# A decoder trunk on one core: the products' moving operands stored as two runs, even columns and odd columns, and read in turn

## The chip, the cores and the metric

The kernel runs on one core of one Trainium2 chip. The metric is the device time of one execution in microseconds (us); less is better. The kernel before takes 568.06 us (median of 3 runs, 568.05 to 568.49).

## What is computed

Two transformer layers on 256 rows of 1024 features. Layer 0 has full causal attention with 16 heads (with one block of 256 keys the block selection selects nothing beyond the own block), layer 1 has 16 query heads on 4 shared key/value heads, a window of 128 and a learned sink. Each layer ends with a gated feed-forward part with a causal convolution of width 3.

```python
for l in range(DEPTH):                       # DEPTH = 2
    h = rmsnorm(x, attn_norm[l])
    ...                                      # q, k, v = h @ w...; rotary; attention -> o
    x = x + o @ w_o
    x = x + conv_ffn(rmsnorm(x, ffn_norm[l]), w_up[l], conv_w[l], conv_b[l], w_down[l])
return rmsnorm(x, final_norm)

def conv_ffn(h, w_up, conv_w, conv_b, w_down):
    u = h @ w_up                             # 1024 -> 2 x 2816
    up = jnp.pad(u, ((0, 0), (CONV_W - 1, 0), (0, 0)))
    u = conv_b + sum(conv_w[j] * up[:, j:j + S_] for j in range(CONV_W))
    gate, val = jnp.split(u, 2, axis=-1)
    return (jax.nn.silu(gate) * val) @ w_down
```

All data are float32, and so is the output.

## The kernel before, in words

**Products in three parts.** Every projection is made from operands split in two: `hi` is the value rounded to the type fp32r, `lo` what is left. A product of x and w is three matmuls that add up in one PSUM bank: x_hi w_hi, x_hi w_lo, x_lo w_hi. Each matmul has a stationary operand of 128x128, which TensorE loads before it, and a moving operand that it reads column by column.

**Weights.** The host packs all weights into 90 units of 128x2048 (`pack`, L1041), in the order of use. A unit is fetched by one DMA on SP (`fetch`, L151), rounded to `wh` by ScalarE (`hi_part`, L156-157), and its rest `wl` taken by VectorE (`lo_part`, L159-160), each in two or four pieces. `prepare` (L166) spreads these pieces over the planned time; `used(i)` (L188) starts unit i+4, and a unit's last step starts the fetch of unit i+3. Weight and activation tiles that TensorE reads come from `spaced` (L79), which begins each 4 elements into its tile.

**Who moves and who is stationary.** In four kinds of product the weights move and activations are stationary: `proj` (L310-323; q, k, v of layer 0 and k/v of layer 1 with 512 columns, the q groups of layer 1 with 256), `v_first` (L733-740, the first block), `Down.mm` (L521-539; attention output and feed-forward down, 512 columns), and `Down.end` (L579-597; the very last unit, in pieces of 256 columns). In the feed-forward up product (`mm` inside `ffn`, L614-630) it is the other way round: a 128x128 piece of `w_up` is stationary and the activations of all 256 rows, features on the partitions, move (256 columns). These activations are `hT` for the first `n_raw` = 4 units and `hS` for the rest.

**Where the moving activations come from.** After a block of the residual stream is final, `feats` (L260-288) transposes it with TensorE into PSUM, ScalarE copies it with the norm's gain into `y` (L276), and VectorE makes `hi` and `lo` from it (L279, L280). For the feed-forward part `feats` is called with `keep=y`; the rows' scale (`rb`) isn't known yet, so units 0 to 3 work with unscaled activations (`hT`) and scale the result, while `scale_x` (L632-643) multiplies `y` by `rb` on VectorE and splits it again into `hS`. Without `keep`, the result is a stationary operand for `proj`.

**Order.** The program's order is written by hand with a planned clock: `tick(ns)` (L116) adds the planned time of the products just issued, counted as columns / 2.4 ns each, and runs the ScalarE and VectorE steps that have come due; `chain` (L124) enqueues such steps, and `require` (L136) forces them before their result is used. In the attention parts the projections of later head groups and of the attention output are fed in as filler between the scores.

Of the kernel before, what the change touches and what calls it, by code (L numbers as in the profile page):

```python
# [60 lines left out]
def trunk(ctx: ExitStack, tc, x, xw, pos, cpk, fin, sinks, w, out):  # L61
# [37 lines left out]

    def half(n):  # L100
        return slice(n * 512, (n + 1) * 512)

# [155 lines left out]
    def feats(b, n, sets, key, keep=None):  # L260

        ts = [bank("t"), bank("t")]
        for j in range(4):
            nc.tensor.transpose(ts[j // 2][:, (j % 2) * P:(j % 2 + 1) * P],
                                xr[b][:, (4 * n + j) * P:(4 * n + j + 1) * P], ident)
        tick(450)

        def steps(hT, g, y, m):
            c = slice(2 * m, 2 * m + 2)
            hi, lo = (part[:, c, blk(b)] for part in hT[n])  # L270
            y_ = y[:, c]

            def gain():
                for j in range(2):
                    col = g + 4 * n + 2 * m + j
                    nc.scalar.activation(y_[:, j], ts[m][:, j * P:(j + 1) * P], AF.Copy, scale=cp[:, col:col + 1])  # L276

            def parts():
                nc.vector.tensor_copy(hi, y_)  # L279
                nc.vector.tensor_tensor(out=lo, in0=y_, in1=f(hi), op=ALU.subtract)  # L280

            return gain, parts

        for k, (hT, g) in enumerate(sets):
            y = mid().rearrange("p (j t) -> p j t", j=4) if keep is None else keep[n][:, :, blk(b)]
            for m in range(2):
                gain, parts = steps(hT, g, y, m)
                chain(key, (200.0 + 1000.0 * k + 500.0 * m, gain), (500.0, parts))
# [21 lines left out]
    def proj(o, hT, b, wv, units=()):  # L310

        n = o.shape[-1]
        for c in range(KC):
            require("x", b, c // 4)
            xh, xl = hx(hT, c)
            wh, wl = wv(c)
            nc.tensor.matmul(o, xh[:, blk(b)], wh, start=(c == 0), stop=False)  # L317
            nc.tensor.matmul(o, xh[:, blk(b)], wl, start=False, stop=False)  # L318
            nc.tensor.matmul(o, xl[:, blk(b)], wh, start=False, stop=(c == KC - 1))  # L319
            tick(3 * n / 2.4)  # L320
            if units and (c + 1) * len(units) % KC == 0:
                used(units[(c + 1) * len(units) // KC - 1])
            yield 3 * n / 2.4
# [190 lines left out]
    class Down:  # L514
# [6 lines left out]
        def mm(self, i, k, b, cols):  # L521
            if self.acc is None:
                self.acc = [[bank("acc") for _ in range(2)] for _ in range(NB)]
            need(self.u + i)
            self.wait(i)
            hi, lo = wq[self.u + i]
            ph, pl = self.parts[2 * i + k]
            first = i == 0 and k == 0
            end = k == 1 and (i == self.n_u - 1 or i == self.n_u - 2 and self.short and (b, cols[0][0]) == (1, 1))
            for n, c in cols:  # L530
                o = self.acc[b][n][:, c]
                s_ = slice(k * D + n * 512 + c.start, k * D + n * 512 + c.stop)
                nc.tensor.matmul(o, ph[:, blk(b)], hi[:, s_], start=first, stop=False)  # L533
                nc.tensor.matmul(o, ph[:, blk(b)], lo[:, s_], start=False, stop=False)  # L534
            for n, c in cols:
                o = self.acc[b][n][:, c]
                s_ = slice(k * D + n * 512 + c.start, k * D + n * 512 + c.stop)
                nc.tensor.matmul(o, pl[:, blk(b)], hi[:, s_], start=False, stop=end)  # L538
            tick(len(cols) * 3 * (c.stop - c.start) / 2.4)

        def units(self, lo, hi):
            for i in range(lo, hi):
                for k in range(2):
                    for b in range(NB):
                        self.mm(i, k, b, [(n, slice(0, 512)) for n in range(2)])
                        yield 6 * 512 / 2.4
                used(self.u + i)

        def finish(self, i0, after, tail=None, by_half=False):

            last = self.n_u - 1

            def unit(i, b, n):
                for k in range(2):
                    self.mm(i, k, b, [(n, slice(0, 512))])

            if by_half:
                for n in range(2):
                    for b in range(NB):
                        for i in range(i0, self.n_u):  # L560
                            unit(i, b, n)
                        self.add(b, n, after)
            for b in () if by_half else range(NB):
                for n in range(2):
                    for i in range(i0, last):
                        unit(i, b, n)
                    if b and n and tail is not None:
                        self.end(b, n, tail)
                    elif b:
                        unit(last, b, n)  # L570
                        self.add(b, n, after)
                if b == 0:
                    for n in range(2):
                        unit(last, b, n)
                        self.add(b, n, after)
            for i in range(i0, self.n_u):
                used(self.u + i)

        def end(self, b, n, tail):  # L579

            i = self.n_u - 1
            require("x", b, n)
            x_ = xr[b][:, half(n)]
            nc.vector.tensor_tensor(out=x_, in0=self.acc[b][n], in1=x_, op=ALU.add)
            need(self.u + i)
            self.wait(i)
            wh, wl = wq[self.u + i]
            for m in range(2):
                o = bank("u")[:, :S]
                for k in range(2):  # L590
                    ph, pl = (t[:, blk(b)] for t in self.parts[2 * i + k])
                    c = slice(k * D + n * 512 + m * S, k * D + n * 512 + (m + 1) * S)
                    nc.tensor.matmul(o, ph, wh[:, c], start=(k == 0), stop=False)
                    nc.tensor.matmul(o, ph, wl[:, c], start=False, stop=False)
                    nc.tensor.matmul(o, pl, wh[:, c], start=False, stop=(k == 1))
                tick(640)
                tail(m, o)

# [9 lines left out]
    def ffn(layer, u_up, u_dn, hT, y, rb, after, tail=None):  # L608
# [5 lines left out]
        def mm(i, up, cs_):  # L614
            need(u_up + i)
            hi, lo = wq[u_up + i]
            for j in range(2):
                o = up[j]
                for c in cs_:
                    if i < n_raw:  # L620
                        for b in range(NB):
                            require("x", b, c // 4)
                    else:
                        require("y", c // 2)
                    s_ = slice((2 * c + j) * P, (2 * c + j + 1) * P)
                    xh, xl = hx(hT if i < n_raw else hS, c)
                    nc.tensor.matmul(o, hi[:, s_], xh, start=(c == 0), stop=False)  # L627
                    nc.tensor.matmul(o, hi[:, s_], xl, start=False, stop=False)  # L628
                    nc.tensor.matmul(o, lo[:, s_], xh, start=False, stop=(c == KC - 1))  # L629
                    tick(3 * 256 / 2.4)  # L630

        def scale_x(m):  # L632
# [4 lines left out]
            def times():  # L637
                for b in range(NB):
                    require("rb", b)
                nc.vector.tensor_tensor(out=y_, in0=y_, in1=rb.unsqueeze(1).to_broadcast([P, 2, S]), op=ALU.mult)  # L640

            chain(("y", m), (2000.0 + 1000.0 * m, times), (700.0, lambda: nc.scalar.activation(hi, y_, AF.Copy)),
                  (600.0, lambda: nc.vector.tensor_tensor(out=lo, in0=y_, in1=f(hi), op=ALU.subtract)))
# [89 lines left out]
    def v_first(c):  # L733
# [2 lines left out]
        wh, wl = (t[:, s_] for t in wq[c // 4])  # L736
        for k, (a, m) in enumerate(((xh, wh), (xl, wh), (xh, wl))):
            for b in range(NB):
                nc.tensor.matmul(v_acc[b], a[:, blk(b)], m, start=(c == 0 and k == 0), stop=(c == KC - 1 and k == 2))  # L739
        tick(1280)  # L740

    def v_out(b, n, o):
# [298 lines left out]
def pack(inp):  # L1041
# [3 lines left out]
    def k_major(m):  # L1045
        return m.reshape(m.shape[0] // P, P, m.shape[1])

    units = []
    m = k_major(inp["w_qkv_a"][0])
    q, k, v = (m[:, :, i * D:(i + 1) * D] for i in range(3))  # L1050
    qk = [np.concatenate([q[:, :, g * 256:(g + 1) * 256], k[:, :, g * 256:(g + 1) * 256]], axis=2) for g in range(4)]
    blocks = [v[:, :, :512], qk[0], qk[1], qk[2], v[:, :, 512:], qk[3]]

    def halves(blk):
        for a in range(2):
# [2 lines left out]
    def rows2(mat):  # L1058
        mm = k_major(mat)
        for i in range(mm.shape[0] // 2):  # L1060
            units.append(mm[2 * i:2 * i + 2].transpose(1, 0, 2).reshape(P, UNIT))

    def up(mat):
        mm = k_major(mat).reshape(KC, P, 2, NF, P)
# [5 lines left out]
    rows2(inp["w_o_a"][0])  # L1070
    up(inp["w_up"][0])
    rows2(inp["w_down"][0])
    halves(k_major(inp["w_kv_b"]))

    order = [(2 * (j // 4) + e) * 4 + j % 4 for j in range(NH // 2) for e in range(2)]
    m = k_major(inp["w_q_b"][0].reshape(D, NH, HD)[:, order].reshape(D, D))
    for g in range(4):
        units.append(m[:, :, g * 256:(g + 1) * 256].transpose(1, 0, 2).reshape(P, UNIT))
    rows2(inp["w_o_b"][0].reshape(NH, HD, D)[order].reshape(D, D))
    up(inp["w_up"][1])  # L1080
    rows2(inp["w_down"][1])
# [41 lines left out]
```

## Time and profile before

| what | value |
|---|---|
| device time, median of 3 | 568.06 us |
| profiled execution: span from first to last instruction | 565.9 us |
| around that span, to the median | 2.2 us |
| TensorE matmul busy | 558.0 us, 3858 matmuls |
| VectorE busy | 427.7 us |
| ScalarE busy | 379.6 us |
| GpSimd busy | 101.6 us |
| mean granted TensorE clock | 0.996 |
| weight fetches | 90 of 1024 KB, 4.8 us from issue to landing |

How to read it: matmuls are pipelined, so the time of one row (for example 275 ns) is longer than the distance between the starts of two of them (about 113 ns in the same place). What a stream of products costs is read from the starts, and this distance is called the pitch below. The profile's rows give a shape as partitions x elements and the number of times after an x; a row of waits names who waited, for whom, and how long in all.

### The profile page before, as it was taken

What the parts mean: (1) busy time and instruction counts of PE and PEld (TensorE: products, weight loads), DVE (VectorE), ACT (ScalarE), POOL (GpSimd) and SP (SyncE); (2) the same over time, 40 slices, a digit from 0 to 9 for tenths busy, and PEclk for the clock granted to TensorE, in tenths of its full rate; (3) what the DMA queues carried; (4) which work ended last, traced back from release to release, by engine and by line L of the source; (5) the groups of instructions that cost most, each with busy time, mean ns of one, the idle gap of its engine ahead of it and who ended that gap; (6) DMA issues with size and microseconds to landing.
All of it is one profiled execution on the core that took longest, in us unless ns stands there. A gap on an engine that the chain in (4) does not pass through costs nothing.

```text
span 565.9 us, 10192 instructions
## 1 busy us (share of the span) xinstructions
PE 558.0 (99%) x3858; PEld 504.4 (89%) x3858; DVE 427.7 (76%) x928; ACT 379.6 (67%) x768; POOL 101.6 (18%) x124
## 2 busy tenths in 40 slices
PE   9999999999999999999999999999999999999995
PEld 7888888899999999988888988889999999988884
DVE  6798678589798888755369988788888888873414
ACT  6988777578577776743449798877657777664213
POOL 7321001012323222100001000002332333110003
PEclk9999999999999999999999999999999999999998
DMA  8974344442566566555542724142465555765201
GB/s 328 371 281 155 145 149 150 149 149 76 197 215 204 213 215 224 207 199 189 216 156 85 289 76 150 74 150 76 149 250 197 206 203 204 254 215 213 85 0 74
DMA packets 15311, 100.99 MB, mean 178 GB/s; under 512 B 1952, under 2 KB 2080, under 8 KB 3744
## 3 DMA queue, kind: packets, MB, share of 16 engines
q1 hardware_dynamic: 14976, 100.09, 49.4%
q8 instruction: 30, 0.49, 0.3%
q10 hardware_dynamic: 288, 0.26, 0.1%
q14 instruction: 17, 0.14, 0.1%
HBM read 99.30 MB, written 1.05 MB: 177 GB/s over the span
## 4 chain that ended last, share of the span: by engine, by line
PE 93%; ACT 3%; DVE 3%; issue 1%; POOL 0%; DVEq 0%; POOLq 0%; ACTq 0%
PE acc L533 9%; PE acc L534 9%; PE acc L538 9%; PE u L628 6%; PE u L627 6%; PE u L629 6%; PE t L628 6%; PE t L629 6%; PE t L627 6%; PE acc L317 4%; PE acc L319 4%; PE acc L318 4%; PE acc L739 2%; PE acc L627 2%; PE acc L628 2%; PE acc L629 2%
## 5 line engine op out<-in xcount | busy, mean ns | idle before, releaser
L160 DVE TENSOR_TENSOR wl<-wr,wh 128x1024 fp32r<-128x1024 f32 (+1 forms) x208 | 222.2, 1086 | 65.9 <-ACT wh L157 65.4
L157 ACT ACTIVATE wh<-wr 128x1024 fp32r<-128x1024 f32 (+1 forms) x208 | 189.8, 946 | 69.7 <-PE acc L538 55.5
L671 POOL TENSOR_TENSOR m<-m,m 128x256 f32<-128x256 f32 x44 | 64.7, 1470 | 176.3 <-DVE m L666 129.0
L533 PE MATMUL acc<-wh,q 128*128 128x512 f32 x238 | 94.5, 397 | 0.2 <-ACT q L492 0.2
L534 PE MATMUL acc<-wl,q 128*128 128x512 f32 x238 | 92.9, 391 | 0.0
L627 PE MATMUL u<-q,wh 128*128 128x256 f32 x320 | 88.4, 277 | 0.0
L628 PE MATMUL u<-q,wh 128*128 128x256 f32 x320 | 88.2, 276 | 0.0
L629 PE MATMUL u<-q,wl 128*128 128x256 f32 x320 | 88.0, 275 | 0.0
L629 PE MATMUL t<-q,wl 128*128 128x256 f32 x288 | 79.2, 275 | 0.0
L627 PE MATMUL t<-q,wh 128*128 128x256 f32 x288 | 79.2, 275 | 0.0
L628 PE MATMUL t<-q,wh 128*128 128x256 f32 x288 | 79.2, 275 | 0.0
L538 PE MATMUL acc<-wh,q 128*128 128x512 f32 x238 | 77.1, 389 | 0.0
L628 PEld LDWEIGHTS u<-q,wh 128*128 128x128 f32 x320 | 60.1, 188 | 0.0
L629 PEld LDWEIGHTS u<-q,wl 128*128 128x128 f32 x320 | 60.1, 188 | 0.0
L627 PEld LDWEIGHTS u<-q,wh 128*128 128x128 f32 x320 | 59.9, 188 | 0.0
L317 PE MATMUL acc<-wh,q 128*128 128x512 f32 (+1 forms) x160 | 57.1, 357 | 0.0
L319 PE MATMUL acc<-wh,q 128*128 128x512 f32 (+1 forms) x160 | 55.4, 346 | 0.0
L318 PE MATMUL acc<-wl,q 128*128 128x512 f32 (+1 forms) x160 | 55.2, 345 | 0.0
L627 PEld LDWEIGHTS t<-q,wh 128*128 128x128 f32 x288 | 54.1, 188 | 0.0
L628 PEld LDWEIGHTS t<-q,wh 128*128 128x128 f32 x288 | 54.1, 188 | 0.0
L629 PEld LDWEIGHTS t<-q,wl 128*128 128x128 f32 x288 | 54.1, 188 | 0.0
L533 PEld LDWEIGHTS acc<-wh,q 128*128 128x128 f32 x238 | 44.7, 188 | 9.7 <-ACT q L492 0.7
(167 smaller groups left out, 991.3 us busy)
## 6 DMA issues: line engine op xcount, KB each, us to landing
wr<-in_w SPq DMA_DIRECT2D x90, 1024.0 KB, 4.8
first<-in_xw SPq DMA_DIRECT2D x5, 384.0 KB, 5.6
xr<-in_x SPq DMA_DIRECT2D x2, 512.0 KB, 8.2
first<-in_xw SPq DMA_DIRECT2D x1, 768.0 KB, 7.0
fin_t<-in_fin SPq DMA_DIRECT2D x1, 512.0 KB, 6.0
out<-ot SPq DMA_DIRECT2D x1, 512.0 KB, 2.6
first<-in_xw SPq DMA_DIRECT2D x1, 388.0 KB, 3.5
out<-m ACTq DMA_DIRECT2D x1, 256.0 KB, 2.1
```

What stands on the lines that cost most here:

```text
L157: nc.scalar.activation(wq[i][0][:, c], raws[i][:, c], AF.Copy)
L160: nc.vector.tensor_tensor(out=wq[i][1][:, c], in0=raws[i][:, c], in1=f(wq[i][0][:, c]), op=ALU.subtract)
L317: nc.tensor.matmul(o, xh[:, blk(b)], wh, start=(c == 0), stop=False)
L318: nc.tensor.matmul(o, xh[:, blk(b)], wl, start=False, stop=False)
L319: nc.tensor.matmul(o, xl[:, blk(b)], wh, start=False, stop=(c == KC - 1))
L533: nc.tensor.matmul(o, ph[:, blk(b)], hi[:, s_], start=first, stop=False)
L534: nc.tensor.matmul(o, ph[:, blk(b)], lo[:, s_], start=False, stop=False)
L538: nc.tensor.matmul(o, pl[:, blk(b)], hi[:, s_], start=False, stop=end)
L627: nc.tensor.matmul(o, hi[:, s_], xh, start=(c == 0), stop=False)
L628: nc.tensor.matmul(o, hi[:, s_], xl, start=False, stop=False)
L629: nc.tensor.matmul(o, lo[:, s_], xh, start=False, stop=(c == KC - 1))
L671: nc.gpsimd.tensor_tensor(out=h, in0=gs, in1=t[1], op=ALU.mult)
```

## The change

The moving operands of all projections get another order in memory: of n columns that one product reads, the n/2 even ones lie first, then the n/2 odd ones. The product's access pattern then takes one element of the first run, one of the second, and so on, so that the columns come in their old order and land in PSUM where they did. The number, sizes and order of all instructions stay.

```diff
+    def turns(t, n=None, at=0):
+        t = t.rearrange("p (a i) -> p i a", a=2)
+        return t if n is None else t[:, at // 2:(at + n) // 2]
+    def pairs(o):
+        return o.rearrange("p (i a) -> p i a", a=2)
+    def turned(t, b):
+        return t.rearrange("p c (a b i) -> p c a b i", a=2, b=NB)[:, :, :, b]
...
-            hi, lo = (part[:, c, blk(b)] for part in hT[n])
+            hi, lo = (part[:, c, blk(b)] if keep is None else turned(part[:, c], b) for part in hT[n])
...
-                    nc.scalar.activation(y_[:, j], ts[m][:, j * P:(j + 1) * P], AF.Copy, scale=cp[:, col:col + 1])
+                    t = ts[m][:, j * P:(j + 1) * P]
+                    nc.scalar.activation(y_[:, j], t if keep is None else t.rearrange("p (i a) -> p a i", a=2), AF.Copy,
+                                         scale=cp[:, col:col + 1])
...
+        o = pairs(o)
...
-            wh, wl = wv(c)
+            wh, wl = (turns(t) for t in wv(c))
...
+            for o, s_ in part:
+                nc.tensor.matmul(o, ph[:, blk(b)], turns(hi[:, s_]), start=first, stop=False)
+                nc.tensor.matmul(o, ph[:, blk(b)], turns(lo[:, s_]), start=False, stop=False)
+            for o, s_ in part:
+                nc.tensor.matmul(o, pl[:, blk(b)], turns(hi[:, s_]), start=False, stop=end)
...
-                    xh, xl = hx(hT if i < n_raw else hS, c)
+                    xh, xl = (turns(t) for t in hx(hT if i < n_raw else hS, c))
...
-                nc.vector.tensor_tensor(out=y_, in0=y_, in1=rb.unsqueeze(1).to_broadcast([P, 2, S]), op=ALU.mult)
+                r = rb.rearrange("p (i a) -> p a i", a=2).unsqueeze(1).to_broadcast([P, 2, 2, P])
+                ya = y_.rearrange("p c (a i) -> p c a i", a=2)
+                nc.vector.tensor_tensor(out=ya, in0=ya, in1=r, op=ALU.mult)
...
-                nc.tensor.matmul(v_acc[b], a[:, blk(b)], m, start=(c == 0 and k == 0), stop=(c == KC - 1 and k == 2))
+                nc.tensor.matmul(pairs(v_acc[b]), a[:, blk(b)], turns(m), start=(c == 0 and k == 0), stop=(c == KC - 1 and k == 2))
```

`Down.end` reads pieces of 256 columns out of a 512-column block in the same way. The host puts the weights in the new order: `pack` gets a function `turns(m, n=512)` that is applied to the q, k, v, k/v and output and down weights (to the q groups of layer 1 with n = 256); the up weights are stationary and stay as they are. The feed-forward activations get the order on the chip: with `keep`, the ScalarE copy out of the transposes (L276) reads every other column from PSUM and writes runs of 64; `scale_x` reads `rb` at every other column. Transposes, scores, the attention's products with v, and their operands are not touched.

More of the change, by code (lines that the diff above doesn't have):

```diff
@@ L284, in feats @@
         for k, (hT, g) in enumerate(sets):
-            y = mid().rearrange("p (j t) -> p j t", j=4) if keep is None else keep[n][:, :, blk(b)]
+            y = mid().rearrange("p (j t) -> p j t", j=4) if keep is None else turned(keep[n], b)
             for m in range(2):
@@ L528, in mm @@
             first = i == 0 and k == 0
[L529 to L539, printed above, removed]
+            end = k == 1 and (i == self.n_u - 1 or i == self.n_u - 2 and self.short and (b, cols[0]) == (1, 1))
+            part = [(pairs(self.acc[b][n]), slice(k * D + n * 512, k * D + (n + 1) * 512)) for n in cols]
+            for o, s_ in part:
[3 more added lines that the diff above has]
+                nc.tensor.matmul(o, pl[:, blk(b)], turns(hi[:, s_]), start=False, stop=end)
+            tick(len(cols) * 3 * 512 / 2.4)
         def units(self, lo, hi):
@@ L544, in units @@
                     for b in range(NB):
-                        self.mm(i, k, b, [(n, slice(0, 512)) for n in range(2)])
+                        self.mm(i, k, b, range(2))
                         yield 6 * 512 / 2.4
@@ L554, in unit @@
                 for k in range(2):
-                    self.mm(i, k, b, [(n, slice(0, 512))])
+                    self.mm(i, k, b, [n])
             if by_half:
@@ L591, in end @@
                     ph, pl = (t[:, blk(b)] for t in self.parts[2 * i + k])
[L592 to L595, printed above, removed]
+                    c = slice(k * D + n * 512, k * D + (n + 1) * 512)
+                    h_, l_ = (turns(t[:, c], S, m * S) for t in (wh, wl))
+                    nc.tensor.matmul(pairs(o), ph, h_, start=(k == 0), stop=False)
+                    nc.tensor.matmul(pairs(o), ph, l_, start=False, stop=False)
+                    nc.tensor.matmul(pairs(o), pl, h_, start=False, stop=(k == 1))
                 tick(640)
@@ L617, in mm @@
             for j in range(2):
-                o = up[j]
+                o = pairs(up[j])
                 for c in cs_:
@@ L1046, in k_major, with turns @@
         return m.reshape(m.shape[0] // P, P, m.shape[1])
+    def turns(m, n=512):
+        return m.reshape(*m.shape[:-1], -1, n // 2, 2).swapaxes(-1, -2).reshape(m.shape)
     units = []
@@ L1051, in pack @@
     qk = [np.concatenate([q[:, :, g * 256:(g + 1) * 256], k[:, :, g * 256:(g + 1) * 256]], axis=2) for g in range(4)]
-    blocks = [v[:, :, :512], qk[0], qk[1], qk[2], v[:, :, 512:], qk[3]]
+    blocks = [turns(t) for t in (v[:, :, :512], qk[0], qk[1], qk[2], v[:, :, 512:], qk[3])]
     def halves(blk):
@@ L1060, in rows2 @@
         for i in range(mm.shape[0] // 2):
-            units.append(mm[2 * i:2 * i + 2].transpose(1, 0, 2).reshape(P, UNIT))
+            units.append(turns(mm[2 * i:2 * i + 2]).transpose(1, 0, 2).reshape(P, UNIT))
     def up(mat):
@@ L1072, in pack @@
     rows2(inp["w_down"][0])
-    halves(k_major(inp["w_kv_b"]))
+    halves(turns(k_major(inp["w_kv_b"])))
     order = [(2 * (j // 4) + e) * 4 + j % 4 for j in range(NH // 2) for e in range(2)]
@@ L1077, in pack @@
     for g in range(4):
-        units.append(m[:, :, g * 256:(g + 1) * 256].transpose(1, 0, 2).reshape(P, UNIT))
+        units.append(turns(m[:, :, g * 256:(g + 1) * 256], 256).transpose(1, 0, 2).reshape(P, UNIT))
     rows2(inp["w_o_b"][0].reshape(NH, HD, D)[order].reshape(D, D))
```

## The prediction

> **What bounds the kernel now.** I read the page's sums first, then who TensorE waited for, then the starts of single products, and last the stages.
>
> ```profile
> span 565.9 us, 10192 instructions
> PE 558.0 (99%) x3858; PEld 504.4 (89%) x3858; DVE 427.7 (76%) x928; ACT 379.6 (67%) x768; POOL 101.6 (18%) x124
> PE   9999999999999999999999999999999999999995
> PEclk9999999999999999999999999999999999999998
> ```
>
> TensorE (PE) is busy in every slice up to the last and its clock is granted in full. The view of waits, for TensorE alone, has three rows in all:
>
> ```profile
> PE u L251 <- DVE warm L227: 1.1, 1, 1.1
> PE t L358 <- DVE m L352: 0.4, 1, 0.4
> PE acc L533 <- ACT q L492: 0.2, 1, 0.2
> ```
>
> That is 1.7 us of 566. So the time is the number of products times their pitch (the distance between two starts), and only a shorter or longer pitch moves it. The timeline of TensorE gives the pitch. First the feed-forward up product, 256 moving columns; the first and the last of 28 products in a row:
>
> ```profile
> 149.83 0.28 PE L629 MATMUL t<-q,wl 128*128 128x256 f32 x1
> ...
> 152.89 0.28 PE L629 MATMUL u<-q,wl 128*128 128x256 f32 x1
> ```
>
> 27 steps in 3.06 us: 113.3 ns. Then the down product, 512 columns, the first and the last of 19:
>
> ```profile
> 260.46 0.39 PE L533 MATMUL acc<-wh,q 128*128 128x512 f32 x1
> ...
> 264.54 0.39 PE L533 MATMUL acc<-wh,q 128*128 128x512 f32 x1
> ```
>
> 18 steps in 4.08 us: 226.7 ns, twice 113.3. So the cost is all per column, 0.4427 ns, and nothing per instruction shows. What a column could cost is seen in the plain f32 work, from the chain of waits in a window at the start (warm-up products, 128 columns) and over the whole span (eight transposes in a row, 128 columns):
>
> ```profile
> 1.90 2.35 PE u L251 x11
> ```
> ```profile
> 30.08 0.87 PE t L358 x8
> ```
>
> The warm-ups take 2.35/11 = 213.6 ns. The code plans 1/2.4 = 0.4167 ns a column (L320); 213.6 is 512 such times, so I read it as four turns per column without a stall. The transposes take 108.8 ns, 256 such times (106.7) and 2.1 ns. The three-part products, which take each column once, need 113.3 = 272 column times for 256 columns, and 226.7 = 544 for 512: one lost in 16. The array, its clock and the writing into PSUM are the same in the warm-ups, which lose none; what differs is that there a new 4-byte column is needed only every fourth turn. So I take the loss to lie in reading the moving operand, one column time per 16 columns or 64 bytes, and it is this reading that the change rearranges.
>
> That the reading isn't a fixed cost shows in one place: the q groups of layer 1, the same three lines and the same shape, run for a while after a break at another pitch:
>
> ```profile
> 314.10 0.28 PE L317 MATMUL acc<-wh,q 128*128 128x256 f32 x1
> ...
> 316.47 0.28 PE L319 MATMUL acc<-wh,q 128*128 128x256 f32 x1
> ```
>
> 20 steps in 2.37 us: 118.5 ns, 28 lost times instead of 16.
>
> **The change part by part: the products.** How many there are stands in the groups by line and shape (the second and third line of each loop have the same counts):
>
> ```profile
> L533 PE MATMUL acc<-wh,q 128*128 128x512 f32 x238 | 94.5, 397 | 0.2 <-ACT q L492 0.2
> L627 PE MATMUL u<-q,wh 128*128 128x256 f32 x320 | 88.4, 277 | 0.0
> L627 PE MATMUL t<-q,wh 128*128 128x256 f32 x288 | 79.2, 275 | 0.0
> L317 PE MATMUL acc<-wh,q 128*128 128x512 f32 x96 | 38.5, 401 | 0.0
> L627 PE MATMUL acc<-q,wh 128*128 128x256 f32 x96 | 25.8, 275 | 0.0
> L317 PE MATMUL acc<-wh,q 128*128 128x256 f32 x64 | 18.6, 291 | 0.0
> L739 PE MATMUL acc<-wh,q 128*128 128x512 f32 x32 | 9.1, 405 | 0.0
> L739 PE MATMUL acc<-wl,q 128*128 128x512 f32 x16 | 4.9, 389 | 0.0
> L593 PE MATMUL u<-wh,q 128*128 128x256 f32 x4 | 1.1, 276 | 0.0
> ```
>
> With 512 columns 3 x 238 + 3 x 96 + 48 = 1050, with 256 columns 3 x (320 + 288 + 96) + 3 x 64 + 3 x 4 = 2316. At 226.7 and 113.3 ns they make 238.0 + 262.4 = 500.4 us of the span. All of them get the new reading.
>
> No row of the trace shows a moving operand read from two places in turn, so its price is bounded. Below: every column costs its one time and nothing else, 213.3 and 106.7 ns; gain 1050 x 13.4 + 2316 x 6.6 = 14.1 + 15.3 = 29.4 us. Above: each column is a step to another place and costs what now only every 16th does, one time more; that is the slow rival below. Between them I take the row of the transposes: it is the nearest stream of products that each load a new stationary operand and lose nothing per 16, and it keeps 2.1 ns per instruction, which may now be hidden under the stall. So 215.4 and 108.8 ns; gain 1050 x 11.3 + 2316 x 4.5 = 11.9 + 10.4 = 22.3 us. I take the gain's side because the loss grows with the columns and not with the instructions or the loads, because the warm-up row excludes the array, and because the 118.5 ns row shows that it depends on how reads fall.
>
> [...]
>
> **What takes some of it back.** A faster TensorE needs its weights and copies sooner. The stages, busy time by engine:
>
> ```profile
> core 0: us, PE busy (x) PEld busy (x) DVE busy (x) ACT busy (x) POOL busy (x), PEclk, DMA share, GB/s
> 30.00:120.00 90.00, 89.95 (x535) 74.28 (x534) 69.53 (x194) 69.14 (x164) 8.92 (x17) 1.00 0.47 166
> 120.00:240.00 120.00, 120.00 (x1049) 119.56 (x1048) 103.40 (x177) 84.46 (x141) 32.94 (x23) 1.00 0.55 190
> 290.00:380.00 90.00, 89.39 (x611) 75.97 (x610) 78.01 (x268) 76.18 (x223) 3.80 (x6) 1.00 0.38 138
> ```
>
> In feed-forward up VectorE has 103.4 us of work in 120; with products at 108.8 the stage is 115.2 and VectorE stands at 90%, the fetches at 190 x 120/115.2 = 198 GB/s, under rates that the page shows elsewhere. The attention of layer 1 (290 to 380) is the tight one: 78.0 us of VectorE and 76.2 of ScalarE in 90, in bursts, and TensorE already has gaps there. Its ten weight units (24 products of 512 columns, or 48 of 256, each) would gain some 2.6 us; I count half of that and some in the other attention as lost, 2 us (0 to 4).
>
> The side work: counts stay, only access patterns change. In the groups by line:
>
> ```profile
> L276 ACT ACTIVATE y<-t,cp 128x128 f32<-128x128 f32 x32 | 9.4, 411 | 0.5 <-PE t L264 0.5
> L280 DVE TENSOR_TENSOR q<-y,q 128x256 fp32r<-128x256 f32 x16 | 6.3, 417 | 0.0
> L640 DVE TENSOR_TENSOR y<-y,rb 128x512 f32<-128x512 f32 x8 | 5.5, 683 | 2.3 <-ACT rb L717 2.3
> ```
>
> At worst each of these doubles, 21 us of engine time in all; nearly all of it lies beside products (TensorE waits for none of it now). What isn't covered is the last block's chain at the start of each feed-forward part: two gains, a cast and a subtraction before its first products. Doubled gains would be 0.8 us there, twice 0.8 = 1.6 at worst and nothing at best, since other blocks' products are ready; I take 0.5. Nothing is added that waits, no queue changes, the DMAs are the same.
>
> **The sum.** 565.9 - 22.3 + 2 + 0.5 = 546.1 us of span. The profiled execution's span leaves 2.2 us to the median of the runs, which I keep: 548.3, forecast **548 us**. With the bounds of its terms this case reaches from 565.9 - 29.4 + 2.2 = 538.7 to about 553.
>
> **The rivals.** *Only part of the stall goes (555 to 559 us).* The two runs lie 128 or 256 columns apart, both whole multiples of 16; so both cross a boundary of 16 columns at the same moment. If two such crossings share one lost time, half the stall goes: 1050 x 6.7 + 2316 x 3.3 = 14.7 us, less 2 to 2.5 us as above: about 556. Or the weight loads are the next bound for 256 columns:
>
> ```profile
> L628 PEld LDWEIGHTS u<-q,wh 128*128 128x128 f32 x320 | 60.1, 188 | 0.0
> L358 PEld LDWEIGHTS t<-ident,m 128*128 128x128 f32 x52 | 6.0, 140 | 2.6 <-issue 0.8 <-DVE m L352 0.6 <-ACT wh L157 0.2
> ```
>
> A load for a three-part product takes 188 ns against 140 for the transposes that run at 108.8. Loads overlap, so neither is a pitch; but if the longer kind can't come closer than 113.3, only the 512-column products gain, 11.9 us, and the time is 558. Against both: 113.3 is exactly half of 226.7.
>
> *Nothing changes (568 to 570 us).* The stall belongs to taking one 4-byte column per time, wherever it lies. Then pitches stay, and up to 1.6 us of side work may show. For it: it is the same in every stage. Against: the 118.5 ns row, where equal products read at another rate.
>
> *Slower: every column pays the step (about 1010 us).* Now 1 step in 16 goes to another 64 bytes and costs one time; read in turn, all do. Then a column costs two times: 240 more lost per 256 columns, 100 ns, and 200 ns per 512: 1050 x 0.2 + 2316 x 0.1 = 441.6 us, so about 1010. It decides as soon as the turns cost more than the 6.6 ns that 256 columns lose now. For it: contiguous reading loses so little that something must help neighbours. Against: nothing in the trace shows a reader that holds only one place. [...]
>
> **How the numbers follow.** Full gain 0.45 (548), part of it 0.23 (556), nothing 0.12, slower 0.20. The measurement can tell about 0.2%, 1.1 us. The range leaves out only the slow rival: from 538 (the full gain's lower end) to 569.5 (nothing changes, some side work). The likeliest case alone has 538 to 553.
>
> **What would show it.** Right: starts of the up products 108 to 110 ns apart and of the down products 214 to 217, TensorE still 98% busy, some waits of TensorE for VectorE or ScalarE between 290 and 380 us of the old span. Partly right: 110 to 113 in one of the two. Wrong: pitches unchanged, or above 113.3 and 226.7, and then the span grows with the number of columns while VectorE and ScalarE fall idle. The groups of L276 and L640 show what side work costs: 411 and 683 ns if strides are free there.

## The result, and the profile after

| | before | after |
|---|---|---|
| device time, median of 4 | 568.05 us | 555.18 us |
| lowest to highest | 568.01 to 568.49 | 554.82 to 555.59 |
| ratio, 95% interval | | 0.9771, [0.9757, 0.9785] |
| span of the profiled execution | 565.9 us | 552.8 us |

The kernel became 12.9 us faster. The forecast was 548 us within 538 to 569.5, and faster at 0.68. The measured 555.2 us is 7.2 us above it, outside the 538 to 553 of its likeliest case and at the price of the partial rival (555 to 559). The page after, its sums and the shares of the chain that ended last (before: PE 93%, ACT 3%, DVE 3%):

```profile
span 552.8 us, 10193 instructions
PE 543.1 (98%) x3858; PEld 500.4 (91%) x3858; DVE 427.9 (77%) x928; ACT 378.9 (69%) x768; POOL 107.2 (19%) x124
PE 85%; DVE 7%; ACT 5%; issue 1%; DMA 1%; POOL 0%; DVEq 0%; POOLq 0%; ACTq 0%
```

The work is the same in number, TensorE's busy time is 14.9 us shorter, and VectorE and ScalarE now hold 12% of the chain instead of 6%: TensorE is still the bound, but less alone. The timeline of TensorE in the places shown before, first the up product (256 columns, the first and the last of 30 products), then the down product (512 columns, the first and the last of 19):

```profile
149.74 0.28 PE L640 MATMUL u<-q,wh 128*128 128x256 f32 x1
...
152.98 0.28 PE L642 MATMUL t<-q,wl 128*128 128x256 f32 x1
```
```profile
260.64 0.38 PE L547 MATMUL acc<-wh,q 128*128 128x512 f32 x1
...
264.53 0.38 PE L547 MATMUL acc<-wh,q 128*128 128x512 f32 x1
```

29 steps in 3.24 us are 111.7 ns (before 113.3, forecast 108.8); 18 steps in 3.89 us are 216.1 ns (before 226.7, forecast 215.4). So the 512-column products came down as forecast, and the 256-column ones by only a third of it: by the prediction's own signs this is "partly right". The loads of stationary columns, by group, got longer from 188 to 192 ns where they belong to the 256-column products, and less (189) where 512 columns follow:

```profile
L641 PEld LDWEIGHTS u<-q,wh 128*128 128x128 f32 x320 | 61.4, 192 | 0.0
L547 PEld LDWEIGHTS acc<-wh,q 128*128 128x128 f32 x238 | 45.0, 189 | 7.2 <-ACT q L507 0.8 <-issue 0.7
```

Two side rows, the gain and the product with the row scale (before 411 and 683 ns):

```profile
L289 ACT ACTIVATE y<-t,cp 128x128 f32<-128x128 f32 x32 | 9.4, 410 | 0.2
L655 DVE TENSOR_TENSOR y<-y,rb 128x512 f32<-128x512 f32 x8 | 6.0, 755 | 2.0 <-ACT rb L732 2.0
```

ScalarE reads every other PSUM column at the same price; VectorE pays 72 ns more eight times.

### The profile page after: what moved, and what is told of

Its sections match the earlier page's. It is cut to its first block, busy times and chain, and to the rows that moved or that the text cites. A ratio compares the mean times of both kernels' runs of the same rounds, so it can differ in the third digit from the quotient of the medians.

```text
span 552.8 us, 10193 instructions
## 1 busy us (share of the span) xinstructions
PE 543.1 (98%) x3858; PEld 500.4 (91%) x3858; DVE 427.9 (77%) x928; ACT 378.9 (69%) x768; POOL 107.2 (19%) x124
## 4 chain that ended last, share of the span: by engine, by line
PE 85%; DVE 7%; ACT 5%; issue 1%; DMA 1%; POOL 0%; DVEq 0%; POOLq 0%; ACTq 0%
PE acc L547 9%; PE acc L550 9%; PE acc L548 9%; PE u L640 6%; PE u L642 6%; PE u L641 6%; PE t L640 6%; PE t L642 6%; PE t L641 6%; PE acc L332 3%; PE acc L333 3%; PE acc L334 3%; DVE wl L172 3%; PE acc L754 2%; PE acc L642 2%; PE acc L641 2%
## 5 line engine op out<-in xcount | busy, mean ns | idle before, releaser
L172 DVE TENSOR_TENSOR wl<-wr,wh 128x1024 fp32r<-128x1024 f32 (+1 forms) x208 | 223.3, 1092 | 55.5 <-ACT wh L169 55.1
L686 POOL TENSOR_TENSOR m<-m,m 128x256 f32<-128x256 f32 x44 | 70.2, 1597 | 167.4 <-DVE m L681 81.9
L547 PE MATMUL acc<-wh,q 128*128 128x512 f32 x238 | 92.2, 387 | 0.2 <-ACT q L507 0.2
L548 PE MATMUL acc<-wl,q 128*128 128x512 f32 x238 | 90.6, 381 | 0.0
L550 PE MATMUL acc<-wh,q 128*128 128x512 f32 x238 | 74.6, 379 | 0.0
L642 PEld LDWEIGHTS u<-q,wl 128*128 128x128 f32 x320 | 61.4, 192 | 0.0
L641 PEld LDWEIGHTS u<-q,wh 128*128 128x128 f32 x320 | 61.4, 192 | 0.0
L640 PEld LDWEIGHTS u<-q,wh 128*128 128x128 f32 x320 | 61.3, 192 | 0.0
L332 PE MATMUL acc<-wh,q 128*128 128x512 f32 (+1 forms) x160 | 55.9, 349 | 0.0
L640 PEld LDWEIGHTS t<-q,wh 128*128 128x128 f32 x288 | 55.3, 192 | 0.0
L641 PEld LDWEIGHTS t<-q,wh 128*128 128x128 f32 x288 | 55.3, 192 | 0.0
L642 PEld LDWEIGHTS t<-q,wl 128*128 128x128 f32 x288 | 55.3, 192 | 0.0
L334 PE MATMUL acc<-wh,q 128*128 128x512 f32 (+1 forms) x160 | 54.2, 339 | 0.0
```

The lines of the kernel that those rows point to most:

```text
L172: nc.vector.tensor_tensor(out=wq[i][1][:, c], in0=raws[i][:, c], in1=f(wq[i][0][:, c]), op=ALU.subtract)
L547: nc.tensor.matmul(o, ph[:, blk(b)], turns(hi[:, s_]), start=first, stop=False)
L548: nc.tensor.matmul(o, ph[:, blk(b)], turns(lo[:, s_]), start=False, stop=False)
L550: nc.tensor.matmul(o, pl[:, blk(b)], turns(hi[:, s_]), start=False, stop=end)
L686: nc.gpsimd.tensor_tensor(out=h, in0=gs, in1=t[1], op=ALU.mult)
```

## The experiments

### Which products gain, and what the side work costs

Three kernels each make one part of the change. `only_512` leaves activations and q groups contiguous:

```diff
-        o = pairs(o)
+        o = pairs(o) if n == 512 else o
...
-            wh, wl = (turns(t) for t in wv(c))
+            wh, wl = (turns(t) if n == 512 else t for t in wv(c))
...
-                    xh, xl = (turns(t) for t in hx(hT if i < n_raw else hS, c))
+                    xh, xl = hx(hT if i < n_raw else hS, c)
...
```

> Only the weights that move in products of 512 columns lie as two runs (the few 256-column pieces of the last unit read from them too); feed-forward activations and q groups stay as before. Theory (the 512-column products carry most of the gain, 1050 x 10.8 ns = 11.3 us, of which about 1.7 is lost in attention): 558.5 us, 0.983 of before. Rival (half of the gain is from the 256-column products and the side work costs the rest): 562.

Measured: 559.61 us, 0.9849 [0.9835, 0.9864], so 8.5 us of gain: 11.4 by the pitch (1050 x 10.9 ns) less 2.9 that didn't come. The theory's 558.5 is 1.1 too low, the rival's 562 too high.

`only_256` is the complement: `turns` stays at `n == 256` in `proj` and in the up product, and `Down`, `v_first` and the host's packing of those weights are as before.

> Only the 256-column products read two runs in turn (feed-forward activations and q groups); weights that move with 512 columns stay contiguous. Theory (2316 x 1.65 ns = 3.8 us, held by the weight loads, less under 1 us of waits and side work): 564.7 us, 0.994. Rival (256-column products gain nothing net): 568.

Measured: 564.25 us, 0.9933 [0.9918, 0.9948]: 3.8 us, as the pitch says (2316 x 1.65 ns). 8.5 and 3.8 make 12.3 of the whole 12.9.

`side_only` has the activations in the new layout and every product contiguous:

```diff
-                o = pairs(up[j])
+                o = up[j]
...
-                    xh, xl = (turns(t) for t in hx(hT if i < n_raw else hS, c))
+                    xh, xl = hx(hT if i < n_raw else hS, c)
...
```

> The feed-forward activations are laid out as two runs, but all products read contiguously, so that the positions of the up product come out permuted and the output is not the trunk's. It leaves the side work alone: ScalarE's gain reads every other column from PSUM and writes runs of 64, VectorE's products read the row scale at every other column. Theory: 568 to 568.6 us, L289 (was 411 ns) within 10% of it. Rival (strides double it): gains 0.8 us each, 569.6 us.

Measured: 568.10 us against 568.09, ratio 1.000 [0.9991, 1.001], and L289 at 411 ns. The side work costs nothing that these runs can measure.

### Streams of products alone: what the reading costs

`pitch_forms` keeps only the operands. Each of its lines is one stream of 48 products, and all follow each other. In the code, `pc` picks a 128x128 stationary piece, `mv_of` the moving `hi` or `lo`, and `o2` the place of the columns in PSUM (P = 128, N = 48):

```python
    def two(t, n, d, at=0):      # two runs, d columns apart, in turn
        return t[:, at:at + 2 * d].rearrange("p (a i) -> p i a", a=2)[:, :n // 2]
...
    for i in range(N):
        nc.tensor.matmul(o2(i, 512), pc(st_of(i), i), two(mv_of(i), 512, 256), start=True, stop=True)  # 512_two_256
```

> No trunk is computed: 28 streams of 48 three-part products each, one line a stream, with real weights as operands; its output means nothing and only the pitches count. Theory (one column time is lost at each step to the next 64 bytes, and reading two runs in turn hides it; after that the 256-column products are held by loading 128 stationary columns, 111.6 ns): contiguous 113.3 (256), 170 (384), 226.7 (512); two runs in turn 111.6 (256), 135.4 (320), 162.1 (384), 215.8 (512); with 96 stationary columns instead of 128, two runs of 256 come down to 108.8 and contiguous stays at 113.3; distances 128, 136 and 256 of the runs make no difference. Rival 1 (the 256-column products keep part of the reading stall, because their runs lie only 128 columns apart): distance 256 gives 108.8, 96 stationary columns stay at 111.6, 384 columns come out above 162. Rival 2 (what helps is only that two crossings coincide): runs 136 or 264 apart, not a multiple of 16, lose half as much as contiguous, about 110 and 220, or all of it. Groups of 2 or 4 columns in turn: as two runs by the theory; groups of 16 as contiguous, 226.7. Every second column (step 2) crosses twice as often: 240 by the theory, 213 to 216 if only neighbours matter. [...]

The chain of waits is here a table of streams: start, duration, line, count. Lines 124 to 130 have 256 columns: contiguous, then two runs 128, 256 and 136 apart. Lines 132 to 150 have 512: contiguous, two runs 256 and 264 apart, groups of 2, 4 and 16 columns from either run in turn, four runs, eight runs, every second column, every fourth. Lines 158 and 160 have 256 columns that begin at the tile's start, contiguous and as two runs; in L172 only every fourth column of the stationary tile is loaded, 128 in all, and two runs of 256 move.

```profile
14.79 6.53 PE acc L124 x48
21.32 5.36 PE acc L126 x48
26.68 5.36 PE acc L128 x48
32.04 5.36 PE acc L130 x48
37.40 11.19 PE acc L132 x48
48.59 10.36 PE acc L134 x48
58.95 10.36 PE acc L136 x48
69.31 15.83 PE acc L138 x48
85.14 11.68 PE acc L140 x48
96.82 11.52 PE acc L142 x48
108.34 13.23 PE acc L144 x48
121.57 23.45 PE acc L146 x48
145.03 21.68 PE acc L148 x48
166.71 22.08 PE acc L150 x48
...
221.31 5.68 PE acc L158 x48
226.99 5.36 PE acc L160 x48
232.35 8.43 PE acc L162 x48
240.78 7.80 PE acc L164 x48
248.58 5.24 PE acc L166 x48
...
265.24 11.19 PE acc L172 x48
```

Divided by 48: two runs take 215.8 ns per 512 columns and 111.7 per 256, at all the distances tried. Contiguous takes 233.1 here, more than in the trunk (226.7). Four runs take 275.6, eight 488.5; every second column 451.7, every fourth 460.0. Groups of 16 take 240.0, groups of 4 243.3, groups of 2 329.8; but these three streams (`og`) also write PSUM in such groups, 256 columns apart, so they don't show the reading alone. 384 columns (L162, L164) take 175.6 contiguous and 162.5 as two runs. And two runs of 256 columns with only 96 stationary columns (L166) take 109.2.

L124 is the contiguous stream of 256 columns, and its 136.0 is a mean of two rates. These are the starts of its first, tenth, eleventh and last product:

```profile
14.59 0.42 PE L124 MATMUL acc<-mvh,sth 128*128 128x256 f32 x1
...
16.51 0.31 PE L124 MATMUL acc<-mvh,sth 128*128 128x256 f32 x1
16.66 0.28 PE L124 MATMUL acc<-mvl,sth 128*128 128x256 f32 x1
...
21.04 0.28 PE L124 MATMUL acc<-mvh,stl 128*128 128x256 f32 x1
```

9 steps in 1.92 us are 213.3 ns, 37 steps in 4.38 us are 118.4. So for its first 4.7 us (from 11.86) TensorE worked at little more than half the later rate, although the mean granted clock of this run is 0.998 (and in the kernel before PEclk, the granted clock in the view of stages, reads 1.00 over the warm-ups, 1.10 to 4.90 us). In that time the contiguous stream lost nothing by estimate: 213.3 is exactly twice 256 of the planned column times (106.7). The contiguous price for 256 columns here is 118.3 to 118.4 (L158 and the later part of L124).

So rival 1 falls (distance 256 is no better, 96 stationary columns are), and rival 2 falls (runs 136 and 264 apart gain as much). But the theory falls in part too. It gave 240 ns for every second column, which crosses 64 bytes twice as often, and 451.7 came; and two runs, which step to another place at every column, are the cheapest form here (215.8 per 512). The cost could lie in how often one and the same small piece is used; the next run asks that.

`pitch_forms_2` asks how near the two places may be, with blocks of 2d columns whose halves are read in turn, and how the loads bind:

```python
    def blocks(t, n, d):
        return t[:, :n].rearrange("p (k a i) -> p k i a", a=2, i=d)
```

> No trunk is computed: 25 streams of 48 products, one line a stream; only the pitches count. Theory (columns go in turn to two readers, each reader holds one 16-byte piece, four columns, and loses little when it uses a piece twice, nothing when it uses it four times, much when once): blocks of 2d columns whose halves are read in turn give 227 to 233 ns per 512 columns for d = 2 (as contiguous) and 215.8 for d = 4 and more; runs 257, 258 or 260 apart 215.8; each column taken twice 215.8. Rival (the two runs must lie far apart, in different parts of the memory): d = 4, 8, 16 stay at 226 or above, and only d = 32 or 64 and more reach 215.8. For the loads: with 120, 112, 64 and 32 stationary columns two runs of 256 take 109 to 111 and then 109, and 272 columns with 128 stationary take 115.4 (272 / 2.4 + 2.1) because moving binds again. If the load's floor depends on where the stationary piece begins, one of the offsets 0, 2, 8 or 16 columns gives 109 instead of 111.7; if it is only the number of its columns, all give 111.7. The same stationary piece in all products: 111.7 (it is loaded each time).

Lines 137 to 149: two runs, then blocks with d = 2, 4, 8, 16, 32, 64. Lines 151 to 157: runs 257, 258 and 260 apart, and each column taken twice. Lines 163 to 171: 256 columns with the stationary piece 4, 0, 2, 8 and 16 columns into its tile. Lines 173 to 179: 120, 112, 64 and 32 stationary columns. Line 181: 272 moving columns.

```profile
27.39 10.36 PE acc L137 x48
37.75 11.20 PE acc L139 x48
48.95 10.36 PE acc L141 x48
59.30 10.36 PE acc L143 x48
...
111.11 10.40 PE acc L153 x48
...
131.86 10.36 PE acc L157 x48
...
153.19 5.36 PE acc L163 x48
158.55 5.36 PE acc L165 x48
...
179.99 5.24 PE acc L173 x48
...
195.71 5.24 PE acc L179 x48
200.95 5.56 PE acc L181 x48
```

With d = 2 the 512 columns take 233.3 ns, as contiguous; with d = 4 and all larger they take 215.8. The runs need not be far apart: four columns, 16 bytes, are enough. That is what the two-readers picture predicted, an estimate from the figures of `pitch_forms`: if the columns go in turn to two readers that each hold one piece of four columns, contiguous reading (233.1) uses each piece twice, two runs (215.8) use it four times, every second column (451.7) uses it once. It is a picture that these figures fit; no run shows the readers themselves. (At 258 columns apart it is 216.7, 0.8 ns more.)

The loads: 120 stationary columns give 109.2 ns, and so do 112, 64 and 32; 128 give 111.7, wherever the piece begins. 272 moving columns with 128 stationary ones take 115.8, where moving binds again. Fewer stationary columns also mean fewer rows of output, but L172 of `pitch_forms` changes nothing but where the 128 stationary columns are read, and its pitch is 233.1. So the load sets the pitch there, and 111.7 is the time of loading 128 neighbouring fp32r columns for one product.

### Does the place of the operands matter?

The kernels place TensorE's operands 4 columns into their tiles. Both were run with `SKIP` 0 instead of 4.

> The changed kernel with TensorE's operand tiles beginning at their tile's start instead of 4 columns into it (SKIP 0). Theory (read in turn, the offset no longer matters for moving columns): 555.2 us, pitches 111.7 and 215.9 as in the changed kernel. Rival (the loads, which read contiguously, depend on the offset): 256-column pitch 109 or above 113, 548 or above 560 us.

> The kernel before with SKIP 0: contiguous reading from the tile's start. Theory (a contiguous stream loses more or less with the place, 113.3 to 118.3 and 226.7 to 233.3 ns as the first stream run showed): between 568 and about 585 us, 2316 x 5 + 1050 x 6.6 ns = 18.5 us more if all products go to the higher pitch. Rival (offset plays no part): 568.

Two runs: 555.16 us, 0.9775 [0.9759, 0.9792], the same as with the offset. Contiguous: 570.03 us in one run against 568.04, and its down products take longer in the group's row (397 ns before):

```profile
L533 PE MATMUL acc<-wh,q 128*128 128x512 f32 x238 | 95.2, 400 | 0.1
```

So a contiguous stream depends on its place, a little, and two runs don't. The contiguous kernel ran once, so its 2.0 us are known only roughly.

### Where some of the gain is given back

The pitches say 1050 x 10.9 + 2316 x 1.65 = 15.3 us, and 12.9 came. The forecast had set 2 us for VectorE's load in the attention stages. Two kernels leave out the rotary turn of q and k (`rope` returns at once), one with contiguous products and one with two runs. VectorE's busy time falls by 11.3 and 12.3 us.

> The kernel before without the rotary turn of q and k (four VectorE instructions in each of 18 places, 15.4 us of VectorE, nearly all in the two attention stages); its output is not the trunk's. It is the base for the next run. Theory (the waits of TensorE in attention come from VectorE's load): a little below before, 566 to 567.5 us.

> The changed kernel, also without the rotary turn. Theory (about 3 us of the change's gain are lost to VectorE's load in the attention stages): without these 15.4 us of VectorE work the distance to the run above is 14 to 15.5 us instead of 12.9, so 551.5 to 552.5 us. Rival (the lost part is latency of chains or ScalarE's load): the distance stays at 12.9 us, 553.5 us or more.

Measured: 567.45 us, 0.9984 [0.9975, 0.9993], and 552.71 us, 0.9724 [0.9711, 0.9737]. Between these two kernels the change brings 14.7 us instead of 12.9. The intervals are about 0.8 us wide to either side, so the 1.9 us between them are known to some 1.2 us. The stages show a part of it. Busy time in the attention of layer 1, first the changed kernel, then without the rotary turn:

```profile
283.00:373.00 90.00, 88.39 (x621) 75.95 (x620) 79.31 (x273) 77.72 (x228) 3.83 (x6) 1.00 0.40 141
```
```profile
283.00:373.00 90.00, 89.23 (x636) 77.36 (x635) 75.81 (x240) 79.61 (x233) 4.59 (x7) 1.00 0.38 140
```

TensorE's gaps (90 less the first number) shrink from 1.6 to 0.8 us when VectorE has 3.5 us less to do there. With contiguous products the same stage has 0.6 us of gaps, and 0.1 without the turn, so what the change adds there falls only from 1.0 to 0.7; in the attention of layer 0 it falls from 0.5 to 0.

Leaving out the turn does two things: VectorE has less to do, and the chain from a projection to its transposes gets shorter. These two runs can't tell them apart. In the changed kernel the largest wait of TensorE after the start is for the turn's last instruction:

```profile
PE t L373 <- DVE m L367: 1.2, 4, 0.4
```

If VectorE's load costs, GpSimd, busy there for only 3.83 us of 90, might take it over: `two_runs_rope_pool` has the four instructions of `rope` on GpSimd.

```diff
-        nc.vector.tensor_tensor(out=ta, in0=t[:, :, 0:ROT], in1=c, op=ALU.mult)
+        nc.gpsimd.tensor_tensor(out=ta, in0=t[:, :, 0:ROT], in1=c, op=ALU.mult)
...
```

> The changed kernel with the rotary turn on GpSimd instead of VectorE; the whole trunk is computed. Theory (VectorE's load is what costs in attention, and GpSimd is idle there, 3.8 us busy of 90): 553 to 555 us. Rival (GpSimd is slower and its chain then holds up the scores): 556 us or more.

Measured: 560.61 us, 0.9863 [0.9849, 0.9876], 5.4 us slower than the changed kernel. The rival is right: in the waits of TensorE the transposes after the turn now wait for GpSimd (6.4 us), whose last instruction of the four takes 561 ns where VectorE's took 251:

```profile
PE t L373 <- POOL m L367: 6.4, 11, 1.7
```
```profile
L367 POOL TENSOR_TENSOR m<-rb 128x64 f32<-128x64 f32 (+1 forms) x18 | 10.1, 561 | 1.4
```

This run took load off VectorE (its busy time is 419.3 us instead of 427.9) and made the chain longer, and the chain decided. So the length of the turn's chain costs here; that VectorE's load alone does isn't shown. No version of these beats the changed kernel with the whole trunk computed.

## Why the prediction was right, and where it was off

**The bound.** Right: TensorE's products times their pitch set the time, and the time followed the pitch (15.3 us by the pitch, 12.9 measured).

**The cause of the loss.** Half right. That the loss lies in the reading of the moving columns holds: in `pitch_forms`, with the same array, the same granted clock (0.998 over that run) and PSUM written in the same order, 512 columns take 215.8, 233 or 452 ns by the order of reading alone. The step that failed is "one column time per 16 columns or 64 bytes". What counted was a distance of four columns, 16 bytes (d = 4 took 215.8 ns, d = 2 233.3), and the one in 16 was no constant: contiguous streams ran at 226.7 ns in the trunk and at 233.1 alone. So the argument that a crossing costs one time, and the price of the slow rival built on it, had the wrong mechanism; that the sign came out right was luck as far as it rested on them.

**The warm-ups.** One support was misread. Their 213.6 ns for 128 plain f32 columns were taken as four turns per column without a stall, at the full rate. But the warm-ups are the first 3.8 us of TensorE's work, and `pitch_forms` shows its products at little more than half the later rate in the first 4.7 us (213.3 ns against 118.4). The transposes, of the same shape, take 108.8 later. So the 213.6 are more likely two turns per column at half rate, an estimate from these figures, and the row couldn't exclude the array. The streams do that.

**512 columns.** Right in size: 215.8 to 216.1 against 215.4 ns, with the 2 ns per instruction taken from the transposes.

**256 columns: the mis-sized term.** 10.4 us were forecast (to 108.8 ns), 3.8 came (111.65). 2316 x 2.85 = 6.6 us, and 548.3 + 6.6 = 554.9, nearly the measured 555.2. The partial rival named the cause, the weight loads as the next bound, but set its price at all or nothing of the step. The runs put it in between: 111.7 with 128 stationary columns, 109.2 with 120 or fewer. The argument against it, "113.3 is exactly half of 226.7", showed only that moving bound before, not what would bind next.

**What is given back.** 2 us in attention and 0.5 for side work were set; 15.3 - 12.9 = 2.4 us came. Without the rotary turn 1.9 of it (known to some 1.2) are not lost, so the turn carries most; the step "VectorE's load" is not shown, and the GpSimd run speaks for the length of the turn's chain. The side work carries nothing. The size came out right, its cause only in part.

**The slow rival.** It didn't come for two runs, but its danger is real: every second column costs 451.7 ns and eight runs 488.5, near the 427 that it set for 512 columns. But a new place at each column did not cost by itself: two runs, which step at every column, take 215.8 ns per 512 columns, and contiguous reading takes 10.9 to 17.3 more (226.7 in the trunk, 233.1 alone).

**Nothing changes.** It fell with the pitches.

## What to carry to other kernels

When one engine is busy all the time, compare the distance between its starts with what the same engine does elsewhere in the trace, and look first whether that other place ran at the same rate: the first microseconds here did not (213.3 against 118.4 ns). A loss in proportion to the columns came here from the order in which they are read, and a layout removed it (226.7 to 216.1 ns for 512 columns). In these runs fp32r columns went fastest when read from two places in turn, 4 or more columns apart (215.8); every second column (451.7), four runs (275.6) and eight runs (488.5) were much worse than contiguous (233.1). Before counting on a new pitch, ask what the stationary load allows: the gain ended there, at 111.7 ns.

## What the runs showed of the hardware that was not expected

- The order of 512 fp32r columns sets their price between 215.8 ns (two runs, or blocks of 8 read in halves) and 488.5 ns (eight runs).
- Each column read twice in a row, or blocks whose halves, 4 columns apart, are read in turn, cost the same 215.8 ns as runs 256 apart. Only halves 2 columns apart cost as much as contiguous reading (233.3).
- The two-readers picture, which no run shows directly, fits contiguous, two runs, blocks, every second column and eight runs. It doesn't give the sizes of all: four runs (275.6) and groups of 2 (329.8) cost less than every second column (451.7), though each reader changes its piece at every use in all three. Whether something holds several pieces there stays open, and so does what the groups' writing to PSUM costs.
- Loading 128 stationary fp32r columns takes 111.7 ns, 2.5 ns more than the 256-column product that covers it (109.2); 120 columns are already hidden (109.2). Taken from every fourth place, 128 take 233.1.
- In the stream kernel TensorE's first 4.7 us run at little more than half the later rate (213.3 against 118.4 ns), with a mean granted clock of 0.998, and contiguous reading loses nothing in that time by estimate (twice 256 planned column times are 213.3).
- Why a contiguous stream runs at 113.3 in one place and 118.3 in another, in the trunk even after a break in the same line (118.5), was not settled. With two runs the difference is gone; but with 256 columns the load holds all of them at 111.7, so only the 512-column streams (215.8 at either place in the tile) show that the reading itself no longer varies.
